# A hybrid S5 and retention layer: S5 chunks further apart and run on beside the output product, the S5 input operand built from loaded rows instead of transposes

## The chip, the cores and the metric

The kernel runs on one core of one Trainium2 chip. The metric is device time in microseconds for one execution of the whole program. Before the change, three runs gave 1434.76, 1433.34 and 1433.36 us, median 1433.36 us.

## The reference, cut to what matters

One layer of a decoder, float32, for 256 prompt positions and 8 sequences of 8 sampled positions (320 columns in all), model width 2048:

```
h = rms_norm(x, norm_mix);  u, q, k, v, g = split(h @ w_in)       # 1024 columns each
# S5 half: 64 groups of 16 channels, a complex diagonal state of 64 each
b_bar = ((exp(lam*dt) - 1) / lam) * b;  bu = u (by group) @ b_bar
x_t = exp(lam*dt) * x_(t-1) + bu_t                                # scan over positions
y = Re(C x) + d*u;  y = gelu(y);  y = y * sigmoid(y @ w_glu + b_glu)
# retention half: 8 heads of 128, rotary q and k, decay gamma_h, chunks of 128
o = groupnorm(retention(q, k, v)) * gn_w;  ret = silu(g) * o
x = x + concat(y, ret) @ w_out                                    # the output product
x = x + (silu(gate) * up) @ w_ffn_out,  gate, up = split(rms_norm(x) @ w_ffn_in)
y = rms_norm(x, norm_final)                                       # and the final states
```

## The kernel before, in words

Every large product keeps float32 accuracy with three passes: a weight block `raw` is loaded, ACT casts it to `hi`, DVE subtracts to get `lo` (`wload`, lines 122 to 135), and TensorE multiplies hi by the high part of the activations, hi by their low part, and lo by the high part (`gemm`, lines 137 to 149). One piece of weights is eight 128x128 blocks, so 24 matmuls of 320 columns; each of `raw`, `hi` and `lo` has three buffers of one piece.

In order of time: four of the 40 column blocks of `w_in` are projected together while x arrives; then the other 36 follow, head by head (q, k, v, g) with an S5 column block (u) between. Beside these projections run two kinds of generators. The retention generators (`head_k`, `head_v`) put transposes, scores and value products of a head between the projection matmuls. The S5 generator (`s5_chunk`, lines 583 to 699) handles one of eight chunks of 128 channels:

- it writes the channels through DRAM (`via`) to get them as `kst`, four neighbouring positions and 16 channels on the partitions, with eight small reads (lines 592 to 596);
- it builds the local input matrix `bl` and the local output matrix `cl` on DVE from b, c and powers of the step (`gpc`, `lpc`), and turns `bl` with four TensorE transposes into `pt`, which ACT copies to `bst` (lines 625 to 630);
- `bst` times `kst` gives `pb`, the input of the scan; `bl` times `cl0` gives `pk_`, copied to `toe` and shifted there by six DMAs (lines 641 to 653);
- DVE scans; then `py` collects `toe` times `kst` and `cl` times the states, `ev` is its sum, goes through DRAM (`back`) and returns as `yc` with eight reads, and the gelu follows in six operations (lines 691 to 697).

Order: TensorE and GpSimd (POOL) run in the order in which the code records them. A model clock `clk` advances with each matmul; a generator yields a delay, and `run_due` resumes it when the clock is there. Chunk c starts at T0 + PER*c of that clock (`start_chunk`), and `DL` holds the delays between its steps. ACT, DVE and SP (which issues the DMAs) are ordered by a scheduler with priorities: weight loads go far ahead, evacuations (`EVAC`) somewhat. Every engine then executes its queue strictly in order.

After the projections the code before drains the clock until chunk 7 is done (line 1026), finishes the S5 states, splits the eight heads' results into high and low parts (`split_r`: heads 0 to 3 into `r4a`, which stands in the S5 pool, heads 4 to 7 into `r4b`, which stands where `xlo`, the low part of the projections' input, was), splits the gelu outputs `u32` into `yhi` and `ylo`, and then runs the output product of the retention half (`ps_o`, 16 column blocks, one piece each). For its first two blocks `gemm_late` takes heads 0 to 3 of both, then heads 4 to 7 of both. After it come the GLU product (`ps_g`, 8 pieces, needs `yhi` and `ylo`), the output product of the S5 half, and the feed-forward part, which is two thirds of the program.

In `rot` (rotary, lines 707 to 720) DVE writes `q_` and `k_`; POOL copies their sampled columns to `qsp` and `ksp`, from which TensorE makes the sampled scores of two heads at once.

Of the kernel before, what the change touches and what calls it, by code (L numbers as in the profile page):

```python
# [12 lines left out]
F32 = mybir.dt.float32  # L13
# [31 lines left out]
def hybrid_kernel(ctx, tc, xT, w_in, w_in4, w_out, w_glu, w_fi, w_fo, vecs, s5p, bc, x0,  # L45
# [204 lines left out]
    csr = mp.tile([P, 2, N], F32, name="csr")  # L250
    kdc = mp.tile([P, H, 2], F32, name="kdc")
    kdt = mp.tile([P, H, NS], F32, name="kdt")
    vs = mp.tile([64, H, P], F32, name="vs")
# [8 lines left out]
    vsp = mp.tile([P, P], F32, name="vsp")  # L262
# [54 lines left out]
    lx0 = s5.tile([P, 2, NPAIR, NB], F32, name="lx0")  # L317
    endp = s5.tile([P, 2, NPAIR], F32, name="endp")
# [166 lines left out]
    def s5_powers():  # L485
        for q in range(2):
            for d in range(2):
                o = lpc[:, :, q, 4 * d:4 * d + 4]
                act.mul(o, lp[:, q].rearrange("p e (c j) -> p c j e", j=4), -1.0 if d > q else 1.0)
                o = gpc[:, :, q, 4 * d:4 * d + 4]  # L490
                act.copy(o[:, :, :, 0], ff[:, q].rearrange("p (c j) -> p c j", j=4))
                act.copy(o[:, :, :, 1:], gp[:, q].rearrange("p e (c j) -> p c j e", j=4))
# [90 lines left out]
    def s5_chunk(c):  # L583
# [21 lines left out]
        shm = [P, 8, CH, 16]  # L605
        for w_, pc in ((0, gpc), (1, lpc)):
            m1, m2 = (s5.tile(shm, F32, name=f"m{q}", tag=f"m{q}", bufs=1) for q in range(2))
            b_ = raw[:, w_].unsqueeze(2).to_broadcast(shm)
            tt(m1, b_, pc[:, c, 0].unsqueeze(3).to_broadcast(shm), MUL)
            tt(m2, b_, pc[:, c, 1].unsqueeze(3).to_broadcast(shm), MUL)  # L610
            if w_ == 0:

                bl = s5.tile([P, 2, 2, 2, CH, 16], F32, name="bl", tag="bl", bufs=1)
                for r, (a, b, op) in enumerate(((m1[:, 0:4], m2[:, 4:8], SUB), (m1[:, 4:8], m2[:, 0:4], ADD))):
                    a, b = (t_.rearrange("p (u q) e h -> p u q (e h)", q=2) for t_ in (a, b))
                    tt(bl[:, r].rearrange("p q u e h -> p u q (e h)"), a, b, op)
# [17 lines left out]
        for i in range(4):  # L634
            for u in range(2):

                for g in range(2):
                    us, gs = slice(64 * u, 64 * u + 64), slice(64 * g, 64 * g + 64)
                    mm(0.04, pb[gs, u, NC * i:NC * i + NC], bst[us, i, gs], kst[us, 2 * (i % 2) + g],
                       start=True, stop=True, tile_position=(64 * u, 64 * g))  # L640
        pk_ = misc("pk_")
        for i in range(2):
            for q in range(2):
                for u in range(2):
                    mm(0.04, pk_[64 * u:64 * u + 64, 32 * i:32 * i + 32],
                       bl[:, q, i, u].rearrange("p e h -> p (e h)"), cl0[:, q, 2 * u + i],
                       start=q == 0, stop=q == 1, tile_position=(0, 64 * u))
        with tc.high_priority(offset=EVAC):
            act.copy(toe[:, :, CH - 1], pk_[:, 0:64].rearrange("p (q h) -> p q h", h=16))
        for u in range(2):  # L650
            for t in range(CH - 1):
                d = 16 * (CH - 1 - t)
                sp.dma_start(toe[64 * u + d:64 * u + 64, :, t], toe[64 * u:64 * u + 64 - d, :, CH - 1])
# [53 lines left out]
    def rot(ps, name):  # L707
        assert rot_t["ready"]
        with tc.high_priority(offset=EVAC):
            return rot_(ps, name)  # L710

    def rot_(ps, name):
# [35 lines left out]
    def head_v(h, v_, qg, rt, R):  # L748
# [8 lines left out]
        act.copy(vsp[64 * (h % 2):64 * (h % 2) + 64], vT[64:128, 2])  # L757
        last = act.copy(vs[:, h], vT[64:128, 2])
        if h == 0:
            rot_t["values"] = last  # L760
            with tc.issue_after(last.ins):
                s5_powers()
            start_chunk(0)
# [8 lines left out]
        if h % 2:  # L772
            two = (HS[h - 1], R)
            mm(0.22, po[:, 2], smp, vsp, start=True, stop=False, skip_group_check=True)
# [86 lines left out]
    def do_q(h, ps=None):  # L861
# [8 lines left out]
        q_ = rot(ps, "q_")  # L870
        pool.tensor_copy(qsp[:, 64 * (h % 2):64 * (h % 2) + 64], q_[:, NP:N])
        qg = qgs[h % 2]
        for u in range(2):
            tt(qg[:, u].rearrange("p (b w) -> p b w", w=40)[:, :, 0:NS],
               q_[:, NP + 32 * u:NP + 32 * u + 32].rearrange("p (b t) -> p b t", t=NS),
               gqt[:, h].unsqueeze(1).to_broadcast([P, 4, NS]), MUL)
# [3 lines left out]
    def do_k(h, ps=None):  # L880
        ps = proj(9 + 4 * h) if ps is None else ps
        R = HS[h]
        k_ = rot(ps, "k_")
        pool.tensor_tensor(kvf[:, h], k_[:, NP:N].rearrange("p (b t) -> p b t", t=NS),
                           kdt[:, h].unsqueeze(1).to_broadcast([P, NB, NS]), MUL)
        pool.tensor_copy(ksp[:, 64 * (h % 2):64 * (h % 2) + 64], k_[:, NP:N])
# [31 lines left out]
    DL = dict(b1=14.2, b2=6.6, scan=17.8, y=10.0, k=8.5, v=6.1,  # L918
              o=2.2, u=6.0, c=10.0, n2=2.4, n2b=2.6, nm=0.8)
    T0, PER = 53.6, 32.0  # L920
# [105 lines left out]
    while "done" not in s5_state:  # L1026
        advance()

    def fin(out, src, m, shape):
# [8 lines left out]
    newscr(2)  # L1038
    finp = s5.tile([P, 2, NPAIR], F32, name="finp", tag="m0", bufs=1)
    fins = s5.tile([P, 2, NPAIR, NB], F32, name="fins", tag="m1", bufs=1)  # L1040
    fin(finp.unsqueeze(3), [endp[:, r].unsqueeze(2) for r in range(2)],
        [tabl[:, r].unsqueeze(2) for r in range(2)], [P, NPAIR, 1])
    fin(fins, [ends[:, 0, r] for r in range(2)],
        [lp[:, r, CH - 1].unsqueeze(2).to_broadcast(shx) for r in range(2)], shx)
    tt(fins, fins, ends[:, 1], ADD)
    sp.dma_start(s5p_o, finp)
    sp.dma_start(s5s_o, fins)

# [10 lines left out]
    def split_r(t_, h):  # L1059
        with tc.high_priority(offset=EVAC):  # L1060
            act.copy(t_[:, 0], retp[:, h])
            tt(t_[:, 1], retp[:, h], f(t_[:, 0]), SUB)
        rhi.a.append(t_[:, 0])
        rlo.a.append(t_[:, 1])

    r4a = s5.tile([P, 4, 2, N], F32R, name="r4a", tag="tab", bufs=1)
    for h in range(4):
        while not ("sg" in HS[h] and "gn" in HS[h]):
            advance()
        split_r(r4a[:, h], h)  # L1070
    rpool = ExitStack()
    rpl = rpool.enter_context(tc.tile_pool(name="rpl", bufs=1, reuse_waits="tile"))
    r4b = rpl.tile([P, 4, 2, N], F32R, name="r4b")
    for h in range(4, H):
        while not ("sg" in HS[h] and "gn" in HS[h]):
            advance()
        split_r(r4b[:, h - 4], h)
    while clk.heap:
        advance()
    s5stack.close()  # L1080

    gl = ExitStack()
    glp = gl.enter_context(tc.tile_pool(name="glp", bufs=1, side="right", reuse_waits="tile"))
    yhi = glp.tile([P, 8, N], F32R, name="yhi")
    ylo = glp.tile([P, 8, N], F32R, name="ylo")
    for c in range(8):
        act.mul(yhi[:, c], u32[:, c], 0.5)
        stt(ylo[:, c], u32[:, c], 0.5, f(yhi[:, c]), MUL, SUB)
    for n in range(KT):
# [3 lines left out]
        tt(x1[:, n], x1[:, n], ps, ADD)  # L1093
    rpool.close()
    zhi = glp.tile([P, 8, N], F32R, name="zhi")
    zlo = glp.tile([P, 8, N], F32R, name="zlo")
    for n in range(8):
        ps = gemm("ps_g", w_glu[n], 8, yhi, ylo)
        with tc.issue_after(last_raw[0].ins):
            sp.dma_start(vd[:, :, n].rearrange("h t e -> t h e"), vs[NS * n:NS * n + NS])  # L1100
# [148 lines left out]
def _host(inp):  # L1249
# [31 lines left out]
    def pairs(k, tr):  # L1281
# [5 lines left out]
                          for p in ("s5_b_", "s5_c_")], 2))  # L1287
    x0 = np.stack([g("state_s5_re")[0], g("state_s5_im")[0]], 0)
# [55 lines left out]
```

## Time and profile before

| | |
|---|---|
| median of three runs | 1433.36 us (1433.34 to 1434.76) |
| the profiled execution | 1433.95 us, of it 1432.1 us span |
| TensorE | 10394 matmuls, busy 1418.1 us |
| DVE, ACT, POOL | busy 954.6, 598.8, 125.1 us |
| DMA | 266.87 MB, 185 GB/s over the span |

The span runs from the first to the last instruction of the program; the 1.85 us beside it lie around it. PE busy is the time in which at least one matmul is in flight. The projections last from about 5 to 342 us, the output product of the retention half from 344 to 400 us, the GLU product from 400 to 429 us, then the S5 half's output product, and the feed-forward part from about 488 us to the end.

### The profile page before, as it was taken

The numbers are of one execution on the slowest core, as the hardware profiler recorded it, in microseconds if no ns is written. First come the engines' busy times: TensorE is split into PE (matmuls) and PEld (weight loads), VectorE is DVE, ScalarE is ACT, GpSimd is POOL, SyncE is SP. The second block draws the span as 40 slices with busy tenths as digits, with TensorE's granted clock in tenths as the row PEclk, the third lists the DMA queues.
The fourth block names the chain that finished last, engine by engine and source line by source line (L and its number), as shares of the span: only waits on it lengthen the run. The fifth ranks groups of instructions, "written<-read, shape, count | busy, mean of one in ns | idle before, by whom it ended". The sixth has DMA issues, their size and how long they took to land.

```text
span 1432.1 us, 26209 instructions
## 1 busy us (share of the span) xinstructions
PE 1418.1 (99%) x10394; PEld 1407.6 (98%) x10394; DVE 954.6 (67%) x1853; ACT 598.8 (42%) x944; POOL 125.1 (9%) x193
## 2 busy tenths in 40 slices
PE   9999999999999999999999999999999999999996
PEld 9999999999999999999999999999999999999996
DVE  7978887777567647776677546777644767644554
ACT  7645555554355433333333333333333333333452
POOL 7530022110000010000001000001000000000001
PEclk9999999999999999999999999999999999999998
DMA  8555555556544466675666446757445765444442
GB/s 285 175 172 161 165 167 165 169 160 208 162 156 152 152 210 228 221 250 205 239 217 228 128 150 234 247 202 254 151 152 185 256 225 183 153 127 156 148 148 108
DMA packets 101803, 266.87 MB, mean 186 GB/s; under 512 B 27312, under 2 KB 41776, under 8 KB 101680
## 3 DMA queue, kind: packets, MB, share of 16 engines
q1 hardware_dynamic: 101536, 264.94, 55.7%
q8 instruction: 81, 1.33, 0.4%
q14 instruction: 42, 0.34, 0.1%
q10 hardware_dynamic: 144, 0.26, 0.1%
HBM read 254.24 MB, written 10.52 MB: 185 GB/s over the span
## 4 chain that ended last, share of the span: by engine, by line
PE 71%; DVE 1%; issue 0%; ACT 0%; DVEq 0%
PE ps_fu L144 7%; PE ps_fu L143 7%; PE ps_fo L143 7%; PE ps_fo L144 7%; PE ps_fo L145 7%; PE ps_fu L145 7%; PE ps_fg L144 7%; PE ps_fg L143 7%; PE ps_fg L145 7%; PE ps_o L145 1%; PE ps_o L143 1%; PE ps_o L144 1%; PE ps_g L144 1%; PE ps_g L145 1%; PE ps_g L143 1%; DVE x L178 0%
## 5 line engine op out<-in xcount | busy, mean ns | idle before, releaser
L131 ACT CAST hi<-raw 128x1024 fp32r<-128x1024 f32 (+1 forms) x416 | 402.2, 968 | 697.4 <-PE ps_fo L144 189.0
L133 DVE TENSOR_TENSOR lo<-raw,hi 128x1024 fp32r<-128x1024 f32 (+1 forms) x416 | 467.5, 1124 | 314.9 <-ACT hi L131 312.4
L144 PE MATMUL ps_fo<-alo,hi 128*128 128x320 f32 x704 | 217.5, 309 | 0.0
L143 PE MATMUL ps_fg<-hhi,hi 128*128 128x320 f32 x704 | 217.5, 309 | 0.0
L143 PE MATMUL ps_fo<-ahi,hi 128*128 128x320 f32 x704 | 217.5, 309 | 0.0
L145 PE MATMUL ps_fo<-ahi,lo 128*128 128x320 f32 x704 | 217.5, 309 | 0.0
L144 PE MATMUL ps_fu<-hlo,hi 128*128 128x320 f32 x704 | 217.4, 309 | 0.0
L145 PE MATMUL ps_fg<-hhi,lo 128*128 128x320 f32 x704 | 217.4, 309 | 0.0
L143 PE MATMUL ps_fu<-hhi,hi 128*128 128x320 f32 x704 | 217.4, 309 | 0.0
L144 PE MATMUL ps_fg<-hlo,hi 128*128 128x320 f32 x704 | 217.4, 309 | 0.0
L145 PE MATMUL ps_fu<-hhi,lo 128*128 128x320 f32 x704 | 217.4, 309 | 0.0
L143 PE MATMUL ps_p<-xhi,hi 128*128 128x320 f32 x560 | 177.3, 317 | 0.0
L145 PE MATMUL ps_p<-xhi,lo 128*128 128x320 f32 x560 | 173.0, 309 | 0.0
L144 PE MATMUL ps_p<-xlo,hi 128*128 128x320 f32 x560 | 172.8, 309 | 0.0
L144 PEld LDWEIGHTS ps_fg<-hlo,hi 128*128 128x128 f32 x704 | 132.4, 188 | 0.0
L143 PEld LDWEIGHTS ps_fo<-ahi,hi 128*128 128x128 f32 x704 | 132.4, 188 | 0.0
L143 PEld LDWEIGHTS ps_fu<-hhi,hi 128*128 128x128 f32 x704 | 132.4, 188 | 0.0
L144 PEld LDWEIGHTS ps_fu<-hlo,hi 128*128 128x128 f32 x704 | 132.4, 188 | 0.0
L145 PEld LDWEIGHTS ps_fo<-ahi,lo 128*128 128x128 f32 x704 | 132.4, 188 | 0.0
L145 PEld LDWEIGHTS ps_fu<-hhi,lo 128*128 128x128 f32 x704 | 132.4, 188 | 0.0
L143 PEld LDWEIGHTS ps_fg<-hhi,hi 128*128 128x128 f32 x704 | 132.3, 188 | 0.0
L145 PEld LDWEIGHTS ps_fg<-hhi,lo 128*128 128x128 f32 x704 | 132.3, 188 | 0.0
(441 smaller groups left out, 2066.6 us busy)
## 6 DMA issues: line engine op xcount, KB each, us to landing
raw<-w_fi SPq DMA_DIRECT2D x176, 512.0 KB, 4.1
raw<-w_in SPq DMA_DIRECT2D x79, 512.0 KB, 4.1
raw<-w_fo SPq DMA_DIRECT2D x64, 512.0 KB, 3.5
raw<-w_out SPq DMA_DIRECT2D x32, 512.0 KB, 3.7
hi<-vd SPq DMA_DIRECT2D x32, 512.0 KB, 5.5
lo<-vd SPq DMA_DIRECT2D x32, 512.0 KB, 5.2
raw<-w_fo SPq DMA_DIRECT2D x64, 192.0 KB, 2.4
rt<-r SPq DMA_DIRECT2D x8, 512.0 KB, 5.3
```

The costliest lines, as they stand in the source:

```text
L131: cast = act.copy(hi[:, :m], raw[:, :m])
L133: last_lo[0] = dve.tensor_tensor(lo[:, :m], raw[:, :m], f(hi[:, :m]), SUB)
L143: pe.matmul(ps, hi, xhi[:, k], start=k == 0, stop=False)
L144: pe.matmul(ps, hi, xlo[:, k], start=False, stop=False)
L145: pe.matmul(ps, lo, xhi[:, k], start=False, stop=k == nk - 1)
```

## The change

Four things change; what is computed stays the same.

1. **Spacing and end.** PER goes from 32.0 to 34.5. The code no longer drains the clock before the output product of the retention half: chunk 7 goes on between its matmuls, and as soon as a column block finds it done, `close_s5` finishes the states, closes the S5 pool and makes `yhi` and `ylo`. For that the splits of the heads leave the S5 pool: head 0 goes to the place of `csr`, head 1 to those of `q_` and `k_`, head 2 to those of `v_` and `sw`, and heads 3 to 7 to one tile where `xlo` was.
2. **The operand of the input product.** The four transposes and the copy to `bst` are gone. b is loaded as `btr` with the wanted rows on the partitions, already repeated (`bt`, prepared on the host). The factors are transposed once for all chunks (`s5_rows`: eight ACT copies to `gs`, two TensorE transposes, one ACT copy to `gt`, one write to DRAM `gtd`), and each chunk reads its part as `gtr` with two broadcasting DMAs. Six DVE operations of 256 elements (`s5_bst`) make the operand in place of b. `bl` is still made, since `pk_` uses it.
3. **Row order.** Rows are (channel, place) instead of (place, channel). `kst` takes two DMAs instead of eight, `toe` six as before with a partition step of 4, `back` four instead of one, `yc` four instead of eight.
4. **Retention.** The last addition of `rot` is cut in two: the prompt columns go to `q_` or `k_`, the sampled ones straight to `qsp` or `ksp`, by DVE; the two POOL copies are gone. The sampled values of two heads share one tile, so `vsp` and its copy are gone, and each of the eight writes of the values to DRAM is cut in two.

```diff
+            for e in range(CH):
+                src = gp[:, q, e - 1] if e else ff[:, q]
+                act.copy(gpc[:, :, q, :, CH - 1 - e].rearrange("p c (d j) -> p c d j", j=4),
+                         src.rearrange("p (c j) -> p c j", j=4).unsqueeze(2).to_broadcast([P, 8, 2, 4]))
+
+    def s5_rows():
+
+        gs = s5.tile([P, 2, 2, CH, 8, 2], F32, name="gs", tag="bl", bufs=1)
+        for r in range(2):
+            for e in range(CH):
+                src = gp[:, r, e - 1] if e else ff[:, r]
+                act.copy(gs[:, r, :, CH - 1 - e], src.rearrange("p (c u q) -> p u c q", u=2, q=2))
+        yield DL["rows"]
+        pt = misc("pt")
+        for r in range(2):
+            tr(pt[:, P * r:P * r + P], gs[:, r].rearrange("p u e c q -> p (u e c q)"))
+        gt = s5.tile([P, 2, P], F32, name="gt", tag="gtr", bufs=1)
+        with tc.high_priority(offset=EVAC):
+            act.copy(gt, pt[:, 0:2 * P].rearrange("p (r s) -> p r s", s=P))
+        sp.dma_start(gtd.rearrange("u e c q r s -> (u e c q) (r s)"), gt.rearrange("p r s -> p (r s)"))
+        load_rows(0)
...
+    def load_rows(c):
+        if c < 8:
+            b, g = (s5.tile([P, 2, 2, P], F32, name=n, tag=n, bufs=1) for n in ("btr", "gtr"))
+            sp.dma_start(b, bt[c])
+            for u in range(2):
+                sp.dma_start(g[64 * u:64 * u + 64].rearrange("p q r s -> p (q r s)"),
+                             gtd[u, :, c].rearrange("e q r s -> e (q r s)").unsqueeze(0)
+                             .to_broadcast([16, CH, 4 * P]))
+            rows[c] = b, g
+
+    def s5_bst(c):
+        b, g = rows.pop(c)
+        t_ = s5.tile([P, 2, 2, P], F32, name="bt_", tag="m0", bufs=1)
+        for r in range(2):
+            tt(t_[:, :, r], b[:, :, 1 - r], g[:, :, 1], MUL)
+        for r in range(2):
+            tt(b[:, :, r], b[:, :, r], g[:, :, 0], MUL)
+            tt(b[:, :, r], b[:, :, r], t_[:, :, r], ADD if r else SUB)
+        return b
...
         for i in range(2):
-            for e in range(CH):
-                sp.dma_start(kst[64 * i + 16 * e:64 * i + 16 * e + 16],
-                             via[2 * i:2 * i + 2, :, :, CH - 1 - e].rearrange("q g h c -> h (q g) c"))
+            sp.dma_start(kst[64 * i:64 * i + 64], via[2 * i:2 * i + 2].rearrange("q g h s c -> (h s) (q g) c"))
...
-        bst = s5.tile([P, 4, P], F32, name="bst", tag="bst", bufs=1)
-        pt = misc("pt")
-        for i in range(4):
-            tr(pt[:, P * i:P * i + P], bl[:, i // 2, i % 2].rearrange("p u e h -> p (u e h)"))
-        with tc.high_priority(offset=EVAC):
-            act.copy(bst, pt.rearrange("p (i s) -> p i s", s=P))
+        bst = s5_bst(c).rearrange("p q r s -> p r q s")
...
+        load_rows(c + 1)
...
-        back = drm.tile([2, CH, 16, 2, 2, NC], F32, name="back", tag="back", bufs=2)
-        sp.dma_start(back.rearrange("i t h u g c -> (i t h) (u g c)"), ev.rearrange("p u g c -> p (u g c)"))
+        back = drm.tile([2, CH, 2, 2, 16, NC], F32, name="back", tag="back", bufs=2)
+        for u in range(2):
+            for g in range(2):
+                sp.dma_start(back[:, :, u, g].rearrange("i t h c -> (i t) h c"), ev[:, u, g])
         yc = s5.tile([P, CH, NC], F32, name="yc", tag="yc", bufs=1)
         for j in range(4):
-            for g in range(2):
-                r = 32 * j + 16 * g
-                sp.dma_start(yc[r:r + 16], back[j % 2, :, :, j // 2, g].rearrange("t h c -> h t c"))
+            sp.dma_start(yc[32 * j:32 * j + 32], back[j % 2, :, j // 2].rearrange("t g h c -> (g h) t c"))
...
-        tt(a, a, sw, ADD)
+        tt(a[:, 0:NP], a[:, 0:NP], sw[:, 0:NP], ADD)
+        tt(pair, a[:, NP:N], sw[:, NP:N], ADD)
...
-    T0, PER = 53.6, 32.0
+    T0, PER = 53.6, 34.5
...
-    while "done" not in s5_state:
-        advance()
-
...
-    r4a = s5.tile([P, 4, 2, N], F32R, name="r4a", tag="tab", bufs=1)
-    for h in range(4):
...
+    late = rpl.tile([P, 5, 2, N], F32R, name="r4")
+    for h in range(H):
         while not ("sg" in HS[h] and "gn" in HS[h]):
             advance()
...
+        if h == 0:
+            split_r(mp.tile([P, 2, N], F32R, name="r0", tag="csr", bufs=1), h)
+        elif h < 3:
+            ta, tb = (mp.tile([P, N], F32R, name=n + "r", tag=n, bufs=1)
+                      for n in (("q_", "k_") if h == 1 else ("v_", "sw")))
+            split_r([ta, tb], h)
+        else:
+            split_r(late[:, h - 3], h)
...
         ps = late[n] if n < 2 else gemm("ps_o", w_out[n, :, 8:16], 8, rhi, rlo)
         tt(x1[:, n], x1[:, n], ps, ADD)
+        if not GL and "done" in s5_state:
+            close_s5()
```

How it moves instructions, at three places. First TensorE at the start of the output product (`ps_o`; `r4a` are heads 0 to 3 before, `r_4781`, `q_r` and `v_r` are the high parts of heads 0, 1 and 2 after, `r_4780` those of heads 3 to 7). Before:

```order
L143 MATMUL ps_p<-xhi,hi 128x320
L144 MATMUL ps_p<-xlo,hi 128x320
L145 MATMUL ps_p<-xhi,lo 128x320
L102 MATMUL py<-kst,toe 64x80 x8
L102 MATMUL py<-xp_139,cl_143 64x80 x16
L161 MATMUL ps_o<-r4a,hi 128x320
```

After:

```order
L145 MATMUL ps_p<-xhi,lo 128x320
L161 MATMUL ps_o<-r_4781,hi 128x320
L162 MATMUL ps_o<-r_4781,hi 128x320
L163 MATMUL ps_o<-r_4781,lo 128x320
L161 MATMUL ps_o<-q_r,hi 128x320
L162 MATMUL ps_o<-k_r,hi 128x320
L163 MATMUL ps_o<-q_r,lo 128x320
L161 MATMUL ps_o<-v_r,hi 128x320
L162 MATMUL ps_o<-swr,hi 128x320
L163 MATMUL ps_o<-v_r,lo 128x320
L161 MATMUL ps_o<-r_4780,hi 128x320
L162 MATMUL ps_o<-r_4780,hi 128x320
```

Chunk 7's `py` no longer stands between the last projection and the output product, and the tenth matmul of that product already reads head 3 from the tile in the place of `xlo`. Chunk 7's `pb` now comes 84 large matmuls into the output product, its `py` 219 (of 384).

Second, ACT at the same place (`hi<-raw` is the cast of a weight piece, L1061 before and L1094 after the high part of a head). Before:

```order
L131 CAST hi<-raw 128x1024
L1061 CAST r4b<-retp 128x320 x3
L913 ACTIVATE sg<-sg 128x320
L677 COPY ev<-py 128x320
L1061 CAST r4b<-retp 128x320
```

After:

```order
L711 COPY ev<-py 128x320
L131 CAST hi<-raw 128x1024
L1094 CAST r_4780<-retp 128x320 x4
L948 ACTIVATE sg<-sg 128x320
L1094 CAST r_4780<-retp 128x320
```

The casts of the late heads stand behind the same weight cast as before, but head 3 is now one of them; on DVE, too, the low parts stand behind the `lo` of that piece, before and after.

Third, DVE at the operand of chunk 0, after (before, one ACT copy `bst<-pt` behind four transposes on TensorE made it, and DVE had nothing there):

```order
L133 TENSOR_TENSOR lo<-raw,hi 128x1024
L178 TENSOR_TENSOR k__1155<-ps_p,csr 128x320
L178 TENSOR_TENSOR sw<-sw,csr 128x320
L178 TENSOR_TENSOR bt__1210<-btr,gtr 128x2x128
L178 TENSOR_TENSOR k__1155<-k__1155,sw 128x256
L178 TENSOR_TENSOR ksp<-k__1155,sw 128x64
L178 TENSOR_TENSOR bt__1210<-btr,gtr 128x2x128
L178 TENSOR_TENSOR btr<-btr,gtr 128x2x128
L133 TENSOR_TENSOR lo<-raw,hi 128x1024
```

The products stand between two `lo` subtractions of weight pieces, and three more of the six follow behind the second.

More of the change, by code (lines that the diff above doesn't have):

```diff
@@ L649, in s5_chunk @@
             act.copy(toe[:, :, CH - 1], pk_[:, 0:64].rearrange("p (q h) -> p q h", h=16))
[L650 to L653, printed above, removed]
+        for t in range(CH - 1):
+            for i in range(t + 1):
+                sp.dma_start(toe[i::CH, :, t], toe[i + CH - 1 - t::CH, :, CH - 1])
         with tc.high_priority(offset=2 * EVAC if c == 7 else 0):
@@ L762, in head_v @@
                 s5_powers()
+                spawn(s5_rows())
             start_chunk(0)
@@ L1036, in fin, with s5_end @@
         tt(out[:, 1], u1, u2, ADD)
[L1038 to L1047, printed above, removed]
+    def s5_end():
+        newscr(2)
+        finp = s5.tile([P, 2, NPAIR], F32, name="finp", tag="m0", bufs=1)
+        fins = s5.tile([P, 2, NPAIR, NB], F32, name="fins", tag="m1", bufs=1)
+        fin(finp.unsqueeze(3), [endp[:, r].unsqueeze(2) for r in range(2)],
+            [tabl[:, r].unsqueeze(2) for r in range(2)], [P, NPAIR, 1])
+        fin(fins, [ends[:, 0, r] for r in range(2)],
+            [lp[:, r, CH - 1].unsqueeze(2).to_broadcast(shx) for r in range(2)], shx)
+        tt(fins, fins, ends[:, 1], ADD)
+        sp.dma_start(s5p_o, finp)
+        sp.dma_start(s5s_o, fins)
     class Cols:
@@ L1059, in split_r @@
     def split_r(t_, h):
+        hi_, lo_ = t_ if isinstance(t_, list) else (t_[:, 0], t_[:, 1])
         with tc.high_priority(offset=EVAC):
[L1061 to L1064, printed above, removed]
-    r4a = s5.tile([P, 4, 2, N], F32R, name="r4a", tag="tab", bufs=1)
-    for h in range(4):
+            act.copy(hi_, retp[:, h])
+            tt(lo_, retp[:, h], f(hi_), SUB)
+        rhi.a.append(hi_)
@@ L1068, in hybrid_kernel @@
+        rlo.a.append(lo_)
+    rpool = ExitStack()
+    rpl = rpool.enter_context(tc.tile_pool(name="rpl", bufs=1, reuse_waits="tile"))
+    late = rpl.tile([P, 5, 2, N], F32R, name="r4")
+    for h in range(H):
         while not ("sg" in HS[h] and "gn" in HS[h]):
             advance()
[L1070 to L1077, printed above, removed]
@@ L1089, in hybrid_kernel, with close_s5 @@
+    gl = ExitStack()
+    GL = {}
+    def close_s5():
+        s5_end()
+        s5stack.close()
+        glp = gl.enter_context(tc.tile_pool(name="glp", bufs=1, side="right", reuse_waits="tile"))
+        yhi = glp.tile([P, 8, N], F32R, name="yhi")
+        ylo = glp.tile([P, 8, N], F32R, name="ylo")
+        for c in range(8):
+            act.mul(yhi[:, c], u32[:, c], 0.5)
+            stt(ylo[:, c], u32[:, c], 0.5, f(yhi[:, c]), MUL, SUB)
+        GL.update(p=glp, y=(yhi, ylo))
     for n in range(KT):
@@ L1093, in hybrid_kernel @@
         tt(x1[:, n], x1[:, n], ps, ADD)
+        if not GL and "done" in s5_state:
+            close_s5()
+    while clk.heap:
+        advance()
+    if not GL:
+        close_s5()
+    glp, (yhi, ylo) = GL["p"], GL["y"]
     rpool.close()
@@ L1287, in _host @@
                           for p in ("s5_b_", "s5_c_")], 2))
+    bt = np.stack([pairs("s5_b_" + q, False) for q in ("re", "im")], 0)
+    bt = bt.reshape(2, P, 8, 2, 2, 16).transpose(2, 3, 5, 4, 0, 1)
+    A["bt"] = c(np.broadcast_to(bt[:, :, :, None], (8, 2, 16, CH, 2, 2, P)).reshape(8, P, 2, 2, P))
     x0 = np.stack([g("state_s5_re")[0], g("state_s5_im")[0]], 0)
```

68 lines of the change are left out of this document (29 added, 39 removed).

## The prediction

> **What bounds the kernel now.** First the page's totals:
>
> ```profile
> span 1432.1 us, 26209 instructions
> PE 1418.1 (99%) x10394; PEld 1407.6 (98%) x10394; DVE 954.6 (67%) x1853; ACT 598.8 (42%) x944; POOL 125.1 (9%) x193
> ```
>
> TensorE is idle for 14 us of 1432. So time falls only where TensorE issues less or waits less, and rises only where it issues more or a new wait appears. Then the table by stretch (us, then busy time of PE, PEld, DVE, ACT, POOL):
>
> ```profile
> 40.00:75.00 35.00, 34.94 (x244) 34.68 (x243) 34.03 (x99) 21.09 (x46) 16.85 (x34) 1.00 0.51 165
> 180.00:215.00 35.00, 35.00 (x326) 34.22 (x319) 28.82 (x61) 18.74 (x40) 8.70 (x11) 1.00 0.53 168
> 320.00:355.00 35.00, 34.50 (x314) 33.73 (x314) 25.18 (x51) 16.52 (x33) 2.32 (x8) 1.00 0.61 204
> 380.00:410.00 30.00, 29.67 (x202) 29.40 (x202) 17.50 (x25) 14.10 (x21) 0.00 (x0) 1.00 0.51 153
> ```
>
> The granted clock is 1.00. DVE is the engine to watch: 34.0 of 35 us early on, 28.8 of 35 in the middle of the projections. Third, TensorE's list of waits (us in total, times, longest); it has six, and three lie in what the change touches:
>
> ```profile
> PE py L102 <- DMA toe<-toe: 0.5, 1, 0.5
> PE pss L102 <- POOL ksp L886: 0.5, 1, 0.5
> PE ps_g L144 <- DVE ylo L182: 0.3, 1, 0.3
> ```
>
> So all that can be won is small: these waits, and the transposes.
>
> **The transposes: 3.35 us less.** In TensorE's timeline (start, length, instruction):
>
> ```profile
> 78.14 0.31 PE L144 MATMUL ps_p<-xlo,hi 128*128 128x320 f32 x1
> 78.29 0.31 PE L145 MATMUL ps_p<-xhi,lo 128*128 128x320 f32 x1
> 78.44 0.60 PE L107 MATMUL pt<-ident,bl 128*128 128x128 f32 x4
> 78.79 0.39 PE L143 MATMUL ps_p<-xhi,hi 128*128 128x320 f32 x1
> 79.03 0.30 PE L144 MATMUL ps_p<-xlo,hi 128*128 128x320 f32 x1
> L107 PE MATMUL pt<-ident,bl 128*128 128x128 f32 x32 | 4.8, 272 | 0.0
> ```
>
> Matmuls overlap, so I price a block by starts, not lengths. Two large matmuls start 78.29 - 78.14 = 0.15 us apart (0.147 over a longer stretch). Around the four transposes it is 78.79 - 78.29 = 0.50, and the next step is 0.24: 0.353 + 0.093 = 0.446 us for a block. Eight blocks are 3.57 us. The two new transposes cost half a block, 0.22. Net -3.35 us. The last row's 272 ns each would make 30 x 0.272 = 8.2 us; these lengths overlap their neighbours, so I take the starts.
>
> [...]
>
> **Three waits: 2.18 us less.** Each is priced by starts again, against the same block where it did not wait:
>
> ```profile
> 84.00 0.31 PE L145 MATMUL ps_p<-xhi,lo 128*128 128x320 f32 x1
> 85.90 0.39 PE L143 MATMUL ps_p<-xhi,hi 128*128 128x320 f32 x1
> 246.35 0.31 PE L145 MATMUL ps_p<-xhi,lo 128*128 128x320 f32 x1
> 247.51 0.39 PE L143 MATMUL ps_p<-xhi,hi 128*128 128x320 f32 x1
> 341.71 0.31 PE L145 MATMUL ps_p<-xhi,lo 128*128 128x320 f32 x1
> 343.78 0.42 PE L161 MATMUL ps_o<-r4a,hi 128*128 128x320 f32 x1
> 107.69 0.31 PE L145 MATMUL ps_p<-xhi,lo 128*128 128x320 f32 x1
> 108.92 0.41 PE L143 MATMUL ps_p<-xhi,hi 128*128 128x320 f32 x1
> 402.39 0.31 PE L143 MATMUL ps_g<-yhi,hi 128*128 128x320 f32 x1
> 403.04 0.41 PE L144 MATMUL ps_g<-ylo,hi 128*128 128x320 f32 x1 [0.33 <-DVE ylo L182]
> ```
>
> The scores of heads 0 and 1 waited for POOL's `ksp`: 1.90 us from 84.00 to 85.90, against 1.16 for the same block at 246.35: 0.74. After the change DVE writes `ksp` right behind `k_`; POOL's queue is not in between. Chunk 7's `py` waited for `toe`, because the drained clock put it only 69 large matmuls behind `pb`: 2.07 against 1.23 us in chunk 0, 0.84. Now 135 stand between, 19.8 us; gone. The GLU product waited for `ylo`: 0.65 - 0.15 = 0.50, and 0.10 in the next step: 0.60. In the new ACT order `yhi` starts two weight casts (7 us) earlier, so this goes too, if chunk 7 is back by then.
>
> **A new wait at the start of the output product: 1.43 us more.** Before, heads 0 to 3 were split beforehand and `gemm_late` covered heads 4 to 7 with 24 matmuls, 3.5 us. Now head 3 lies in the place of `xlo`, free only when the projections have ended, and is wanted by the tenth matmul. The queues in front of it, as they are in the run before (ACT twice, then DVE twice):
>
> ```profile
> 342.92 1.03 ACT L131 CAST hi<-raw 128x1024 fp32r<-128x1024 f32 x1
> 343.85 1.18 ACT L1061 CAST r4b<-retp 128x320 fp32r<-128x320 f32 x3
> 344.19 1.23 DVE L133 TENSOR_TENSOR lo<-raw,hi 128x1024 fp32r<-128x1024 f32 x1
> 345.33 0.49 DVE L178 TENSOR_TENSOR r4b<-retp,r4b 128x320 fp32r<-128x320 f32 x1
> ```
>
> Let T be the first matmul of the output product. The cast in front refills the `hi` buffer that the last projection piece but none after it has used, so it starts at about T + 0.1. Head 3's high part follows 0.93 us later and takes 0.46: T + 1.5. DVE subtracts that piece's `lo` first, from T + 1.2, then head 3's low part 1.14 us later, 0.49 long: T + 2.85, with a signal's way T + 2.9. TensorE gets to the first matmul that needs it, the eleventh, at T + 1.47. So 2.9 - 1.47 = 1.43 us. Bounds: 0, if head 3 were early after all; 2.9, if DVE is one weight piece (1.14 us) and a small operation further behind. Behind this wait stands the whole output product, so nothing hides it. Heads 4 to 7 come 12 matmuls (1.8 us) later and are covered.
>
> **The six products per chunk, and chunk 0's way to them: 0.2 us more.** An operation of this size takes 0.42 us, six 2.5 us a chunk, 20 us in all on DVE. The group's row, and for the narrowest place the `lo` of a piece and the cast that starts when TensorE begins with that piece:
>
> ```profile
> L178 DVE TENSOR_TENSOR bl<-m,m x16: 409/420/427, 67.4 to 308.1; 128x256 f32<-128x256 f32 x16
> 68.82 1.22 DVE L133 TENSOR_TENSOR lo<-raw,hi 128x1024 fp32r<-128x1024 f32 x1
> 71.01 1.05 ACT L131 CAST hi<-raw 128x1024 fp32r<-128x1024 f32 x1 [1.53 <-PE ps_p L144]
> 64.75 0.91 ACT L492 COPY gpc<-gp 128x96 f32<-128x96 f32 x4
> ```
>
> That `lo` ends at 70.0 and its piece starts at 71.0: 1.0 us to spare, the least in the projections. The new order helps just there: three operations of chunk 0 that stood in front of that `lo` now stand behind it. In the middle, 28.8 + 2.5 is 31.3 of 35 us, and the wider spacing takes 2.5/34.5 of S5's own work out of each stretch. What hides it is DVE's idle time; without that cover it would be the rival below. The eight copies to `gs` come on ACT right behind `gpc<-gp`, at 0.23 us each or less; they end near 66.6, and TensorE wants them at about 66.8 by its order: between 0 and 1.9 us (all eight late), I take 0.2. `gtr` needs two DMA trips, one behind the other: `gt` is copied by about 68.8 and written at 70.5, 3.6 us later the write has landed, two reads take 0.9 to issue and 3.6 to land, 78.6 us. DVE wants it at about 80.
>
> **The DMAs: 0.** `kst` saves 48 issues in all and `yc` 32; `back` adds 24, b and factors 25, the values 8. SP issues at 0.3 to 0.6 us; what stands behind on SP are weight loads. Landings barely depend on size (KB each, us to landing):
>
> ```profile
> kst<-via SPq DMA_DIRECT2D x64, 20.0 KB, 3.4
> back<-ev SPq DMA_DIRECT2D x8, 160.0 KB, 3.6
> raw<-w_in SPq DMA_DIRECT2D x79, 512.0 KB, 4.1
> ```
>
> For chunk 7, 165 large matmuls (24.2 us) lie between `py` and the GLU product. The way back is `py` 1.2, `ev` 0.9, four issues 1.8, landing 3.6, `yc` issues 0.9 and landing 3.5, gelu 3.4, first `yhi` and `ylo` 1.0: 16.3 us. 7.9 us to spare.
>
> [...]
>
> **Sum:** -3.35 - 2.18 + 1.43 + 0.2 = -3.9 us. On the profiled execution, 1433.95, that is 1430.05; that execution lies 0.6 us above the median of the three runs, so **1429.5 us** against 1433.36. About 0.2% (2.9 us) is what a measurement of this kernel can tell from no change.
>
> **Rivals.**
> - *No new wait* (head 3's place is free earlier, or the `lo` in front is early): -5.3, 1428.1 us. Against it: the order puts both behind the end of the projections. 17%.
> - *The edges are worse*: the wait at head 3 is 2.9, the `gs` copies are all late, 1.9: -0.7, 1432.7 us. For it: 1.0 us to spare at 70 us. 20%.
> - *Chunk 7 is back too late*, and the GLU product takes up the wait that left `toe`: it decides from 7.9 us of lateness on; at 11 us, 3 us of waiting, and `ylo`'s 0.6 isn't won: 1433.1 us. For it: `yc` waits for four `back` writes, and SP carries weight loads between. 5%.
> - *Slower: DVE becomes the bound of the projections.* Place: `lo` behind the six products, chunk for chunk. It decides when a chunk's 2.5 us use up the 1.0 to spare and are not won back before the next: 8 x 1.5 = 12 us, 1429.5 + 12 = 1441.5 us. For it: 34.0 of 35 us at 40 to 75. Against: 28.8 of 35 later. 10%.
> - *Transposes at their recorded length*: -8.7, 1424.7 us. 2%.
>
> The forecast keeps 46%, by itself from 1428.2 to 1431. For 8 in 10 I take **1427.0 to 1433.5**: it leaves out the slow rival and the transposes at full length. Faster by over 0.2% (below 1430.5): nearly all of the forecast, the first rival and the last, 0.62; within 0.2%: the second and third and the forecast's edge, 0.28; slower 0.10.
>
> **What would show it.** Right: 30 transposes fewer and no wait of TensorE for `ksp`, `toe` or `ylo`; one new wait of some 1.4 us of `ps_o` for a head's part in the place of `xlo`, ended by DVE; otherwise no new entry over 0.3 us. Wrong: waits of `ps_p` for `lo`, of `pb` for `btr`, of `ps_g` for `yhi` or `ylo`, or no wait in `ps_o` at all.

## The result and the profile after

The changed kernel takes 1444.26 us (median of six runs, 1441.74 to 1445.65) against 1434.16 us for the kernel before (six runs): ratio 1.0069, 95% interval 1.0056 to 1.0082. It is slower by some 10 us, where 3.9 us less were forecast. The profiled execution of the change took 1444.08 us, 1442.3 of them span.

The page's totals of the changed kernel:

```profile
span 1442.3 us, 26157 instructions
PE 1420.2 (98%) x10364; PEld 1407.3 (98%) x10364; DVE 973.8 (68%) x1917; ACT 591.8 (41%) x937; POOL 111.2 (8%) x177
```

TensorE issues 30 operations less and yet is busy 2.1 us longer; its idle time rises from 14.0 to 22.1 us. The table by stretch says where (us, busy time of PE, PEld, DVE, ACT, POOL, then the granted clock):

```profile
40.00:75.00 35.00, 33.58 (x232) 32.87 (x231) 33.47 (x94) 22.38 (x55) 21.74 (x35) 1.00 0.55 175
180.00:215.00 35.00, 32.66 (x284) 31.67 (x276) 26.63 (x60) 16.62 (x36) 4.83 (x9) 0.95 0.61 191
320.00:355.00 35.00, 31.52 (x258) 29.86 (x259) 29.66 (x63) 16.29 (x37) 3.85 (x8) 0.90 0.47 140
380.00:410.00 30.00, 30.00 (x247) 29.71 (x246) 18.76 (x29) 13.02 (x20) 0.00 (x0) 1.00 0.51 163
```

Before, TensorE was full in the second and nearly full in the third row; now 2.3 and 3.5 us are empty, and the clock is 0.95 and 0.90. DVE is not fuller in the first two rows, 33.47 against 34.03 and 26.63 against 28.82; in the third it is, 29.66 against 25.18, with 5 us of idle time still left. TensorE's waits over 0.5 us (the one for `ones` stands in the kernel before too, with the same 1.1 us):

```profile
PE ps_p L143 <- ACT hi L131: 1.6, 1, 1.6
PE po L102 <- ACT vs L792: 1.6, 1, 1.6
PE po L102 <- ACT vT L791: 1.3, 1, 1.3
PE pss L102 <- ACT toe L684: 1.2, 1, 1.2
PE warm_ps L116 <- POOL ones L62: 1.1, 1, 1.1
PE pt L107 <- ACT gs L501: 1.1, 1, 1.1
PE ps_o L162 <- DVE r L178: 0.9, 1, 0.9
PE ps_p L145 <- DVE lo L133: 0.7, 1, 0.7
```

The waits for `ksp`, `toe` behind its DMAs and `ylo` are gone, as forecast. The head split (`ps_o`, DVE `r`) is there, as forecast. But most of the new entries end on ACT, at unrelated places: a weight cast, a value copy, `toe`. What they share stands in the waits of the other two engines (`gy` is POOL's factor for the group norm of a head, which ACT applies in `on`). In the changed kernel:

```profile
ACT on L839 <- POOL gy L833: 42.1, 7, 7.3
DVE y L182 <- DMA yc<-back: 18.9, 6, 4.7
ACT y L727 <- DVE y L182: 17.0, 6, 4.0
```

Before, there was no wait of DVE for `yc` at all, and ACT's two waits were shorter:

```profile
ACT on L804 <- POOL gy L798: 24.7, 8, 5.5
ACT y L693 <- DVE y L182: 3.2, 4, 2.5
```

`y` of L182 is the first operation of a chunk's gelu, called y1 below; it reads the returned chunk `yc`. One of the six waits (start, length, instruction, and in brackets the idle time before it and its releaser), first in DVE's timeline:

```profile
313.57 0.48 DVE L178 TENSOR_TENSOR k_r<-retp,q_r 128x320 fp32r<-128x320 f32 x1
317.81 0.76 DVE L182 SCALAR_TENSOR_TENSOR y<-u,vec,yc 128x320 f32<-128x320 f32 x1 [3.76 <-DMA yc<-back]
318.49 1.22 DVE L133 TENSOR_TENSOR lo<-raw,hi 128x1024 fp32r<-128x1024 f32 x1
```

ACT's timeline at the same place:

```profile
313.18 1.05 ACT L131 CAST hi<-raw 128x1024 fp32r<-128x1024 f32 x1 [0.98 <-PE ps_p L144]
318.65 0.47 ACT L727 ACTIVATE y<-y 128x320 f32<-128x320 f32 x1 [4.42 <-DMA raw<-w_in]
320.15 0.87 ACT L791 ACTIVATE vT<-pst,rtok 128x128 f32<-128x128 f32 x3
322.70 0.29 ACT L792 COPY vs<-vT 64x128 f32<-64x128 f32 x1
```

And TensorE's:

```profile
320.56 0.94 PE L102 MATMUL po<-vT,sm 128*128 128x128 f32 x6 [1.28 <-ACT vT L791]
323.04 0.79 PE L102 MATMUL po<-vs,smp 128*128 128x128 f32 x2 [1.55 <-ACT vs L792]
326.92 0.47 PE L144 MATMUL ps_p<-xlo,hi 128*128 128x320 f32 x1
327.19 0.47 PE L145 MATMUL ps_p<-xhi,lo 128*128 128x320 f32 x1
```

DVE's next operation is y1; DVE is free for it from 314.0 on and stands until `yc` lands at 317.8. ACT's next operation is the square of y1, so it stands too, 4.42 us (the row names the load of a weight block as releaser; y1 ended 0.08 us before ACT went on). Behind the square stand `vT` and `vs`, which TensorE needs. The last two rows show a second price: behind the stops the large matmuls start 0.27 us apart in place of 0.147; the granted clock from 323 to 329 us is 0.50.

Priced by starts as in the prediction, the stops of the changed kernel are: 66 us (`gs`) 1.4; 189 to 196 us 4.2 with its slow matmuls; 283 us (`toe`) 1.5; 317 to 329 us 6.0 with its slow matmuls; 350 us (head 3) 1.8. Together 14.9 us. Less the 4.9 us that transposes, `ksp` and `toe` were to save, that makes 10.0; from the first value product to the GLU product the trace has 353.84 us against 342.88, 11.0 more. The last 1.0 us I cannot place.

### The profile page after: what moved, and what is told of

It is laid out like the page before. It is cut to its first block, busy times and chain, and to the rows that moved or that the text cites. A ratio compares the mean times of both kernels' runs of the same rounds, so it can differ in the third digit from the quotient of the medians.

```text
span 1442.3 us, 26157 instructions
## 1 busy us (share of the span) xinstructions
PE 1420.2 (98%) x10364; PEld 1407.3 (98%) x10364; DVE 973.8 (68%) x1917; ACT 591.8 (41%) x937; POOL 111.2 (8%) x177
## 4 chain that ended last, share of the span: by engine, by line
PE 92%; DVE 3%; DMA 2%; ACT 2%; issue 0%; SPq 0%; DVEq 0%; ACTq 0%
PE ps_fo L143 7%; PE ps_fu L143 7%; PE ps_fu L144 7%; PE ps_fo L144 7%; PE ps_fo L145 7%; PE ps_fu L145 7%; PE ps_fg L143 7%; PE ps_fg L144 7%; PE ps_fg L145 7%; PE ps_p L143 5%; PE ps_p L145 5%; PE ps_p L144 5%; PE ps_o L143 2%; PE ps_o L144 2%; PE ps_o L145 2%; DVE lo L133 1%
## 5 line engine op out<-in xcount | busy, mean ns | idle before, releaser
L143 PE MATMUL ps_p<-xhi,hi 128*128 128x320 f32 x560 | 178.3, 318 | 1.6 <-ACT hi L131 1.6
```

What stands on the lines that cost most here:

```text
L143: pe.matmul(ps, hi, xhi[:, k], start=k == 0, stop=False)
```

## The experiments

Two theories. **RETURN**: the place of y1 in DVE's order. The planner (the scheduler that orders the queues) seems to put y1 where it expects `yc` to have landed, and with the new return that is earlier; no run separates the four reads from the four writes in this. Counted in weight pieces (`lo`) between `ev` and y1 on DVE, for the eight chunks: before 4 4 4 5 3 5 4 7, after 3 3 4 3 3 2 3 3. **LOAD**: the six products and the spacing fill DVE, the slower rival of the prediction. To these came HEAD, for what the first runs left over.

**E1, the old return in the changed kernel.** Edit:

```diff
-        back = drm.tile([2, CH, 2, 2, 16, NC], ...)
-        for u in range(2):
-            for g in range(2):
-                sp.dma_start(back[:, :, u, g]..., ev[:, u, g])
+        back = drm.tile([2, CH, 16, 2, 2, NC], ...)
+        sp.dma_start(back..., ev...)
         yc = ...
         for j in range(4):
-            sp.dma_start(yc[32 * j:32 * j + 32], back[j % 2, :, j // 2]...)
+            for g in range(2):
+                r = 32 * j + 16 * g
+                sp.dma_start(yc[r:r + 16], back[j % 2, :, :, j // 2, g]...)
```

> The changed kernel with one thing undone: the way of a chunk's output back (one write of ev and eight reads into yc, as before, in place of four writes and four reads). In the order of DVE y1, the operation that takes yc, moves from 2 to 4 weight pieces behind ev back to 4 or 5, as in the kernel before; the spacing of 34.5, the six products and everything else stay. Theory RETURN (in the change y1 stands so early in DVE's order that DVE, and ACT behind it, stand still for yc: 18.9 us of DVE in six waits): these waits go to 0, TensorE's stops at 283 and 317 us go (1.5 us, and 4.8 us with some 1.3 us of slower matmuls behind it), so 7 to 8 us less than the change: 1436 to 1437.5 us, 1.0015 to 1.002 of before. Theory LOAD (the six products and the wider spacing fill DVE and ACT, the place of y1 only shows it): the same waits of TensorE end on other operations, 1442 to 1446 us.

Measured: 1435.58 us, 1.0012 of before (1.0003 to 1.0020), 8.7 us less than the change. DVE's wait for `yc` is gone, and so are the stops at 283 and 317 us. The stop at 189 us went too, which I had not put down to the return. The 8.7 us are a net figure: by starts the stops at 189, 283 and 317 us were 11.7 us and are gone, and the block of `gs` costs 0.3 us in place of 1.4, but the stop at head 3 grew from 1.8 to 5.5 us with the slow matmuls behind it (below).

**E2, the new return in the kernel before.** The same edit the other way round.

> The kernel before with one thing of the change alone: back written by four DMAs and yc read by four. In DVE's order y1 moves from 3 to 5 weight pieces behind ev to 1 to 3 for the first seven chunks. There are no six products here, the spacing is 32. RETURN: DVE waits 10 to 25 us for yc and TensorE stops where ACT's evacuations come late behind it: 3 to 9 us more than before, 1437 to 1443 us. LOAD: without the products there is idle time enough on DVE to take the waits up: within 1.5 us of before, 1433 to 1436 us.

Measured: 1438.96 us, 1.0030 (1.0021 to 1.0039). The planner moved y1 here as well (3 2 2 3 2 2 1 6 pieces), and the list of waits has what was missing before:

```profile
ACT y L693 <- DVE y L182: 14.1, 7, 4.1
DVE y L182 <- DMA yc<-back: 10.3, 6, 3.0
```

So the new return alone, four writes and four reads, costs 4.5 us, with no product and no other spacing in the kernel. TensorE pays it in places of no relation again: 0.7 us for a `lo`, 1.7 us for `r4b`.

**E3, y1 later, the DMAs as in the change.** Edit:

```diff
+        with tc.issue_after(last_lo[0].ins):
             stt(y1..., u32[:, c]..., v("d", c), yc..., MUL, ADD)
-    DL = dict(b1=14.2, b2=6.6, scan=17.8, y=10.0,
+    DL = dict(b1=14.2, b2=6.6, scan=17.8, y=26.0,
```

> The changed kernel with its DMAs as they are, but y1 told to come 16 us later and behind the weight piece in work then: in DVE's order it stands 4 to 7 pieces behind ev instead of 2 to 4, nothing else moves by more than a piece. RETURN: DVE's wait for yc goes to about 0 and the time to that of the changed kernel with the old return, 1436 to 1437.5 us; if that one and this differ, the difference is the DMAs' own (issue time on SP, 4 + 4 against 1 + 8). A rival, DMA (the four writes of eight rows outermost hold the weight loads up on their queue, and the stops come from late weights): no gain here, 1442 to 1446 us.

Measured: 1436.58 us, 1.0016 (1.0007 to 1.0025). The same four writes and four reads, and DVE's wait for `yc` is not in the list. So it is the place of the reader and not the way of the data. With y1 late, the DMAs themselves cost nothing within 1 us (1436.58 against 1435.58 us in E1), which is what the prediction said of them.

**E4, the old spacing in the change.** `PER = 32.0`.

> The changed kernel with the chunks 32 us apart again; y1 stays early in DVE's order (2 to 3 pieces behind ev). Theory SPACING (the wider spacing moves the chunks' work onto the heads' group norms, seen at 189 us, where ACT waited 6.8 us for POOL's gy and TensorE lost some 4 us with the slower matmuls behind): the stop at 189 goes, 3 to 5 us less than the change, 1439 to 1441 us. RETURN: DVE's wait for yc stays at 15 to 25 us and the stops that it causes only change their places: 1441 to 1446 us.

Measured: 1449.70 us, 1.0109 (1.0093 to 1.0124), over the top of either expectation. y1 stands 3 3 2 2 2 3 3 3 pieces behind `ev`, closer still, and DVE's wait grows with it:

```profile
DVE y L182 <- DMA yc<-back: 26.9, 6, 6.1
```

Not all of the longer time need come from there: TensorE's wait at head 3 is 3.7 us here, and `ps_p` waits for `lo` six times, 4.3 us in all. SPACING falls: narrower is worse as long as y1 stands early. Of DVE's waiting a little less than half reaches the end: 4.5 of 10.3 us in E2, 8.7 of 18.9 in the change against E1.

Why 189 us? The statistics of a head's group norm in DVE's timeline of the change:

```profile
183.24 0.75 DVE L178 TENSOR_TENSOR tb<-e,e 128x256 f32<-128x256 f32 x2
183.91 0.49 DVE L822 BATCH_NORM_STATS2 st<-po 128x6 f32<-128x128 f32 x2
```

And in that of E3:

```profile
177.41 1.43 DVE L178 TENSOR_TENSOR e<-e 128x256 f32<-128x256 f32 x4
178.75 0.49 DVE L823 BATCH_NORM_STATS2 st<-po 128x6 f32<-128x128 f32 x2
```

The value product ends at nearly the same time in both (the next large matmul at 179.0 and 178.3). DVE had waited 4.6 us for chunk 1's `yc` at 159.7 and is about 5 us behind 24 us later; POOL's `gy` and ACT's `on` (a wait of 6.79 us) follow it, and behind `on` stand three weight casts. Between 164.2 and 184.4 the trace lists no wait of DVE, so it had no pause in which to catch up. That this backlog is the one from 159.7 is a reading of the two traces; that the stop goes when y1 alone moves is shown by E3.

**What was left: the start of the output product.** E1 still lies 5.5 us over the sum of the prediction. That sum held 1.4 us for head 3; by starts E1 loses 4.2 there, and 1.3 more in eleven slow matmuls behind it, which leaves 1.4 us without a place. DVE's timeline in E1:

```profile
336.71 1.22 DVE L133 TENSOR_TENSOR lo<-raw,hi 128x1024 fp32r<-128x1024 f32 x1
337.84 0.42 DVE L178 TENSOR_TENSOR btr<-btr,gtr 128x256 f32<-128x256 f32 x1
338.18 0.48 DVE L178 TENSOR_TENSOR ev<-ev,py 128x320 f32<-128x320 f32 x1
338.57 0.42 DVE L178 TENSOR_TENSOR btr<-btr,bt__4856 128x256 f32<-128x256 f32 x1
338.91 0.42 DVE L178 TENSOR_TENSOR btr<-btr,gtr 128x256 f32<-128x256 f32 x1
339.36 0.43 DVE L178 TENSOR_TENSOR btr<-btr,bt__4856 128x256 f32<-128x256 f32 x1
339.71 0.48 DVE L178 TENSOR_TENSOR sg<-ps_p,rbc 128x320 f32<-128x320 f32 x1
340.11 1.22 DVE L133 TENSOR_TENSOR lo<-raw,hi 128x1024 fp32r<-128x1024 f32 x1
341.24 0.89 DVE L178 TENSOR_TENSOR r<-retp,r 128x320 fp32r<-128x320 f32 x2
```

TensorE's in E1:

```profile
338.44 0.41 PE L161 MATMUL ps_o<-r,hi 128*128 128x320 f32 x1 [0.43 <-ACT r L1094]
342.18 0.42 PE L162 MATMUL ps_o<-r,hi 128*128 128x320 f32 x1 [3.33 <-DVE r L178]
```

Chunk 7's six products stand in DVE's order in front of the weight piece that stands in front of head 3's low part. The prediction had only the weight piece there. Four runs on this, each on top of E1.

**E5, head 3 elsewhere and the products behind the splits.** Edits:

```diff
-        bst = s5_bst(c).rearrange("p q r s -> p r q s")
+        with tc.issue_after(rot_t["split"].ins) if c == 7 else ExitStack():
+            bst = s5_bst(c)
+        bst = bst.rearrange("p q r s -> p r q s")
...
+        elif h == 3:
+            split_r([mp.tile([P, NP + P], F32R, name=n, tag="mk", bufs=2)[:, 0:N] for n in ("r3h", "r3l")], h)
         else:
-            split_r(late[:, h - 3], h)
+            split_r(late[:, h - 4], h)
```

(`rot_t["split"]` is the last head's subtraction.)

> The changed kernel with the old return, and two edits at the start of the output product: head 3's two parts lie in the two mask buffers (free long before), not in the place of xlo; and the six products of chunk 7 come in DVE's order behind the last head's split, not in front of it. With the old return alone 4.2 us are lost there by starts (0.6 and 3.6), and some 1.3 us behind it in eleven matmuls 0.27 us apart instead of 0.147. Theory HEAD (the start of the output product holds nearly all of what the old return leaves of my error): the waits go, head 4's low part comes at about 339.4 and is wanted at 340.1: 5 to 5.8 us less than 1435.6, 1429.8 to 1430.8 us, about the 1429.5 predicted, and faster than both kernels. Rival (something else ate the saved transposes all along the projections): less than 3 us less, over 1432.5 us.

Measured: 1430.28 us, 0.9971 (0.9961 to 0.9982). Faster than both kernels; HEAD holds.

**E6, head 3 elsewhere alone**, the second of these edits.

> The old return and head 3's place in the mask buffers; chunk 7's products stay in front of the splits in DVE's order. HEAD with the place as its cause: no wait left, 1430 to 1431 us. HEAD with DVE's queue as its cause (products, ev, sg and one weight piece stand in front of whichever head comes first): head 4's low part ends at about 341.7, wanted at 340.2, a wait of about 1.5 us with a little slow matmul behind it: 1432 to 1433.5 us.

Measured: 1432.95 us, 0.9992 (0.9983 to 1.0000). So DVE's queue decides, not the place alone; the wait moves on to head 4. It is 2.6 us and not 1.5:

```profile
PE ps_o L162 <- DVE r L178: 2.6, 1, 2.6
```

**E7, the products behind the splits alone**, the first edit.

> The old return and chunk 7's products behind the last split; head 3 stays in the place of xlo. The queue in front of head 3's low part is then the one that the prediction counted (one cast, one weight piece): a wait of about 1.4 us in place of 3.6 and 0.6 to 0.9, and little slow matmul behind: 1432 to 1433 us. If the place alone were the cause: 1435 to 1436 us, no gain.

Measured: 1432.14 us, 0.9984 (0.9975 to 0.9993). This is the case that the prediction had priced at 1.43 us. DVE's timeline in E7:

```profile
337.67 1.21 DVE L133 TENSOR_TENSOR lo<-raw,hi 128x1024 fp32r<-128x1024 f32 x1
338.81 0.88 DVE L1097 TENSOR_TENSOR r<-retp,r 128x320 fp32r<-128x320 f32 x2
```

TensorE's in E7:

```profile
338.25 0.41 PE L161 MATMUL ps_o<-r,hi 128*128 128x320 f32 x1 [0.43 <-ACT r L1096]
339.74 0.41 PE L162 MATMUL ps_o<-r,hi 128*128 128x320 f32 x1 [1.08 <-DVE r L1097]
```

The output product starts at T = 336.33. Head 3's subtraction ends at 338.81 + 0.48 = 339.29 (0.48 us is the length of a single one), T + 2.96, where the prediction had T + 2.85. But TensorE goes on only when the second subtraction of the pair is done (339.69), 0.05 us behind it, as if one wait covered two heads; E1 and the change show the same 0.05 us behind the second. By starts it is 1.93 us. In E6 TensorE went on at 342.49, when DVE had done the third of its subtractions and not the first, which fits the 2.6.

**E8, the four transposes back**, no `gs`, no rows, no products.

> The old return, and the operand made by four transposes and a copy per chunk again, no gs, no rows, no products. Against the old return alone (1435.6): 8 blocks of 0.45 us more less the first block of two, 0.55: 3.0 us more; the six products no longer stand in front of head 3's low part: 2 to 3.5 us less at the start of the output product. Together 1434.6 to 1436.6 us, the transposes read in the starts of the large matmuls as 0.35 and 0.09 us a block. LOAD (the products cost time all along the projections): less than 1434 us.

Measured: 1443.71 us, 1.0067 (1.0054 to 1.0080), 8 us over E1. The sum missed, and the reason is another accident of the order. Without the products, chunk 7's scan came earlier in DVE's order, in front of the additions that free the output product's accumulators:

```profile
PE ps_o L143 <- DVE x L178: 5.6, 1, 5.6
PE ps_p L145 <- DVE lo L133: 1.9, 2, 1.5
PE ps_o L162 <- DVE r L178: 0.9, 1, 0.9
```

So this run's time doesn't price the products. Its starts do price the transposes: six of the eight blocks take 0.35 us over the pace, as in the prediction, the first and the last 0.46 and 0.59; with 0.09 in each step behind, that is 3.9 us in all, against the 3.57 worked out in the prediction.

**E10, E6 with the spacing of 32.**

> The kernel with the old return and head 3 in the mask buffers, with the chunks 32 us apart in place of 34.5. In DVE's order y1 stands 3 to 5 pieces behind ev; chunk 7's six products stand eleven pieces before the end of the projections and not in front of the splits; each stretch of DVE holds the products 8% closer together. LOAD (the products need the wider spacing): new waits of ps_p for lo in the projections, over 1433 us. RETURN and HEAD (the place of y1 and the queue in front of the splits were all): no such waits, and none at the start of the output product over 0.7 us, 1430 to 1431.5 us, that is 1.5 to 3 us less than with 34.5.

Measured: 1430.89 us, 0.9975 (0.9965 to 0.9984), 2 us less than E6. No wait of `ps_p` in the list; one of 1.0 us in `ps_o` is left, a little over the bound given. LOAD falls: the products fit at the narrower spacing too, when y1 does not stand in the way. With 34.5 E6 loses at the splits what E10 does not; that chunk 7's products stand there is the difference in the order.

**E11, E5 with the two transposes of `gs` later.** `rows=14.0` in place of 11.0.

> The version with both edits at the output product, with the two transposes of gs told to come 3 us later: on TensorE they stand 22 large matmuls further back. With 11 us that block took 0.86 us more than its neighbours' pace in the trace, 0.2 to 0.4 where it didn't wait. If gs alone was late, the block goes to about 0.25 and the time to 1429.3 to 1430 us; if the rows, which come three pieces later then, are late for chunk 0's products, pb waits for btr and the time is 1430.5 us or more.

Measured: 1429.36 us, 0.9963 (0.9951 to 0.9976), with 1427.4 us of span the shortest of all. The wait for `gs` is gone, and none for `btr` came. That it is better than E5 is not shown by the intervals; that it is faster than both kernels is.

## Why the prediction was wrong, point by point

- **The step that failed: "The DMAs: 0".** It priced issues, landings and what stands behind them on SP, and asked for chunk 7 alone whether the return is in time. It never asked where the reader of `yc` stands in DVE's order, with four reads in place of eight. A warning was in the new order beforehand: 3 pieces behind `ev` instead of 4 are 3 x 24 x 0.147 = 10.6 us of matmuls, and the prediction's own price for the way from `ev` to `yc` was 1.8 + 3.6 + 0.9 + 3.5 = 9.8 us, so next to nothing was left. In the trace after, both sides were worse than that. DVE stood ready for y1 already 5.4 to 11.2 us after `ev` in the six chunks that waited, and the return took 9.2 to 12.3 us there: the four writes took 2.6 us to issue, and the last read landed up to 6 us after its issue, where 3.5 were priced. Before, y1 came 14.1 to 26.0 us after `ev` and never waited, so no view of the kernel before could show this. E1, E2 and E3 price the step at 8.7, 4.5 and 7.7 us, net of what else moved with y1.
- **The transposes, -3.35 us: right.** By starts the removed blocks were worth 3.6 to 3.9 us. The recorded lengths (8.2 us) would have been far off.
- **Three waits, -2.18 us: right.** The scores of heads 0 and 1 take 1.02 us over the pace in place of 1.75. From the GLU product to the feed-forward part it is 494.89 - 410.41 = 84.48 us, before 85.08: 0.60 less, as said. `py` of chunk 7 no longer waits.
- **The new wait at head 3, +1.43 us: mechanism right, size off.** In the change it is 0.59 + 1.20 = 1.8 us; with the queue that the prediction assumed, 1.93 (E7). The missing half microsecond is the second subtraction: TensorE went on 0.05 us behind its end, not behind the first (E1, E7 and the change). My upper bound, 2.9, did not hold in E1 (4.2): as the worst queue I had counted one small operation and one weight piece more, and chunk 7's products came into it.
- **Chunk 0's way, +0.2 us: mis-sized, inside its bounds.** In the change the block cost 1.4 us over the 0.22 of an undisturbed one, in E1, E3, E5, E6 and E7 0.2 to 0.6.
- **The slower rival named the right engine and nearly the time, 1441.5 us, by a mechanism that was not there, so the near time is luck.** DVE was not full: E3 and E10 keep every product, and in neither does `ps_p` wait for `lo` (in the change itself it does so once, 0.7 us). DVE stood still at the head of its queue.
- **The other terms of the sum held to about half a microsecond.** From the first value product to the GLU product E11 takes 4.08 us less than before, with half a microsecond of waiting for head 4 still in it; the prediction's terms for that stretch, without the waits that E11 removed, are -3.35 - 0.74 - 0.84 = -4.9. That E11's 1429.36 us lie so near the 1429.5 forecast is in part chance, since E11 has the old return and edits at head 3, at chunk 7's products and at `gs` that the predicted kernel had not.

The stretches with a lower clock (0.57 from 193.0 to 196.4 us, 0.50 from 323 to 329 us) are a cost that the sum had no term for: about 1.3 us at 189 us and 1.1 us at 327 us.

## What to carry to other kernels

When a change makes a transfer cheaper or splits it differently, look in the new order for the instruction that reads it: a planner that believes the data earlier puts the reader earlier, and on an engine that runs its queue in order the whole queue, and the next engine's, waits with it (in the change DVE 18.9 us in six waits for `yc`, ACT 17.0 us in six for y1 behind it). A reader that came late cost next to nothing here, so leave it late (E1 and E3 do it in two ways, at 1435.58 and 1436.58 us against 1444.26, neither with a wait for `yc`). And price a wait with the queue of the new order, not with that of the old trace.

## What the hardware showed

After a stop TensorE ran at about half pace: large matmuls 0.267 us apart in place of 0.147, 7 to 11 of them 0.47 us long in place of 0.31. The granted clock there was 0.57 (193.0 to 196.4 us) and 0.50 (323 to 329 us) in the changed kernel, and 1.00 in the kernel before in the same stretches. In the timeline of the changed kernel:

```profile
195.27 0.47 PE L143 MATMUL ps_p<-xhi,hi 128*128 128x320 f32 x1
195.54 0.47 PE L144 MATMUL ps_p<-xlo,hi 128*128 128x320 f32 x1
195.80 0.38 PE L145 MATMUL ps_p<-xhi,lo 128*128 128x320 f32 x1
196.02 0.31 PE L143 MATMUL ps_p<-xhi,hi 128*128 128x320 f32 x1
```

It followed a wait of 3.33 us in E1 (eleven slow matmuls), waits of 1.65 and 0.69 us and of 1.28 and 1.55 us in the changed kernel (seven each time), and waits of only 0.43 and 1.08 us within 2 us in E7 (eleven); in E6 the two matmuls behind a wait of 2.60 us were 0.64 and 0.47 us long. After 0.35 us in E5 there was none, nor after 1.21 us (`toe`) and after the 0.43 and 0.94 us at head 3 in the changed kernel, nor after 1.48 us at 73 us in E8:

```profile
72.95 0.41 PE L145 MATMUL ps_p<-xhi,lo 128*128 128x320 f32 x1 [1.48 <-DVE lo L133]
73.20 0.31 PE L143 MATMUL ps_p<-xhi,hi 128*128 128x320 f32 x1
73.35 0.30 PE L144 MATMUL ps_p<-xlo,hi 128*128 128x320 f32 x1
```

So a stop can cost 0.8 to 1.3 us more behind it (7 to 11 x 0.12), and the length of one wait alone does not decide whether it does: 1.21 and 1.48 us had no slow matmuls behind them, 0.43 and 1.08 us close together had eleven. What decides it no run here shows.

E3 keeps the four `back` writes and comes within 1 us of E1 with its one write, but there y1 stands so late that a slower write would be hidden. What the four writes add to the return itself no run here shows.
